# The order of two groups of projections at the start of a hybrid mixer: gates and attention values ahead of attention q and k

## The chip, the cores and the metric

The kernel runs on one core of one Trainium2 chip. The metric is device microseconds for one execution. Executions that are only timed give the median that is quoted; a profiled execution leaves a trace and has a time of its own, and the trace covers a span that is a little shorter than that time.

## The reference

The program computes a two-layer encoder trunk on 256 tokens of 1024 features in fp32. A layer is three residual steps, each followed by a LayerNorm: a SwiGLU feed-forward half-step, a mixer, and a second feed-forward half-step.

```python
for l in range(DEPTH):
    x = layer_norm(ALPHA * x + 0.5 * swiglu(x, ffn1_w_gu[l], ffn1_w_down[l]), ln1_g[l], ln1_b[l])
    h = x @ w_in[l]
    dq, dk, dv, mz, mxbc, mdt, gq, gk, gv, gz, gb, ga = jnp.split(h, IN_SPLITS, axis=-1)
    a_out = diff_attention_mixer(dq, dk, dv, cos, sin, da_lambda[l], da_subln_w[l], lambda_init(l))
    m_out = mamba2_mixer(mz, mxbc, mdt, ...)
    g_out = gated_deltanet_mixer(gq, gk, gv, gz, gb, ga, ...)
    mix = jnp.concatenate([a_out, m_out, g_out], -1) @ w_out[l]
    x = layer_norm(ALPHA * x + mix, ln2_g[l], ln2_b[l])
    x = layer_norm(ALPHA * x + 0.5 * swiglu(x, ffn2_w_gu[l], ffn2_w_down[l]), ln3_g[l], ln3_b[l])
```

The mixer has three head groups that read one projection `h`. Differential attention uses q and k (512 columns together) and values dv (256 columns): rotary embedding, two softmax maps per head, their difference times dv, and an RMS norm. The Mamba-2 group and the gated DeltaNet both use decays made from the gates (16 columns: `gb`, `ga`, `mdt`) through a sigmoid, a softplus and cumulative sums. The DeltaNet also needs normalised q and k, and inverts a triangular matrix for each chunk of 64 tokens.

## The kernel before, in words

The 256 tokens are two blocks of 128, b=0 and b=1. The program is six segments (feed-forward, mixer, feed-forward, twice). Each segment is a list of units, and a unit is one tile of weights: it is loaded by DMA from SP's queue into `raw` (5 buffers), split into a rounded high part `wh` on ACT (L265) and a remainder `wl` on DVE (L266) in 7 buffers each, and used on PE in three products, high x high, high x low and low x high. Token-stationary units do these at L357, L358 and L360 for one block at a time; units that serve both blocks at once do them at L342; the output and down projections at L253, L254 and L260.

The mixer's units come from the table `WIN`: each entry names a group of projections and its columns of `w_in`, and the list is worked in the order of the table. The groups `dqk` (512 wide: attention q and k) and `gd` (272 wide: dv and the gates, three DMAs to each part) have four parts each and are token-stationary; `qk0`, `qk1` (DeltaNet q and k), `m00` to `m11` (Mamba-2 x, B, C) and `v` (DeltaNet v) that follow serve both blocks at once; `mz`, `gz` and the output projection close the segment. Over the eight units of `dqk` and `gd`, `order()` lets block 0 run up to `LAG` = 5 units ahead of block 1, since block 1's input is ready later: the norm (L424 to L432) and the transposes `xps` (L275) that make `xT` for block 1 run while PE multiplies block 0.

When a group's last part is done, a generator is started (`spawn`) that issues the work on its result: `after_dqk` (L1018: rotary, transposes `dtps`, scores `scps`, exponentials `sm` at L1064, the sums of probabilities times dv in `dops`, norm into `do`), `after_gd` (L557: copies of dv and gates, then `decays`, L570, a chain of small DVE steps that ends in `a4` at L606, followed by the cumulative sums `csps` on PE and the decay matrices `dps` on PE, L647, with their exponentials `ex` on ACT, L652), and after `qk1` the DeltaNet's `delta`: SiLU of `qk` (L555), squares `sq`, sums `ssps`, `ss` (L693), r = ss^-0.5 on POOL (L695), factors `d` (L717, L718), products `laps` on PE and `LA` = laps x d x ex on DVE (L728). Generators are advanced between the units by their own estimates of time; a scheduler then fixes each engine's order at build time. Every engine works through its own list in that order: an instruction that waits holds all that stand behind it on its engine. The helpers record many operations from one line: L404 is every small matmul, L275 every transpose, L445 a power on POOL. PSUM has two pools of four buffers: `ps` for the units' sums, and `aux`, taken in turn, for all the mixers' small results, so that a new small result waits until the one four before it has been read.

## Time and profile before

| | |
|---|---|
| median of 3 timed executions | 1070.83 us (1070.76 to 1071.52) |
| the profiled execution: its time | 1073.73 us |
| its span in the trace | 1071.9 us, mean granted clock of TensorE 0.994 |
| PE busy | 1046.2 us (98%) |
| DVE busy | 754.8 us (70%) |
| ACT busy | 606.6 us (57%) |
| POOL busy | 30.6 us (3%) |

In the trace, busy time is that of instructions running; a bracket behind a row gives idle time before it and what ended this. Layer 1's mixer lies at about 187 to 357 us of the span, and layer 2's repeats it some 529 us later, wait for wait. In the page's 40 slices every slice but the first and the last has a busy PE share of 9 tenths or more.

### The profile page before, as it was taken

How to read it: one execution, taken by the hardware profiler on the slowest of the kernel's cores; microseconds unless marked ns; L12 is line 12 of the kernel's file. 1: busy time of each engine (PE TensorE's matmuls, PEld its weight loads, DVE VectorE, ACT ScalarE, POOL GpSimd, SP SyncE). 2: the span in 40 equal slices, each digit the busy share in tenths (PEclk: the TensorE clock that was granted, in tenths of full speed). 3: DMA queues.
4: the chain of work that ended last, by engine and by line, in shares of the span. 5: the costliest groups of instructions: out<-in, count | busy, mean ns of one | idle time of the engine just before them, and what ended most of it. 6: DMA issues, size and time to landing. Idle time of an engine off the chain costs nothing.

```text
span 1071.9 us, 17626 instructions
## 1 busy us (share of the span) xinstructions
PE 1046.2 (98%) x6358; PEld 894.5 (83%) x6358; DVE 754.8 (70%) x1554; ACT 606.6 (57%) x1301; POOL 30.6 (3%) x29
## 2 busy tenths in 40 slices
PE   8999999999999999999999999999999999999996
PEld 7888888788887788888878888887888878888885
DVE  6777754887877877774587776457977787777644
ACT  6687643487435566664456666435873445666530
POOL 0000000001001000000000000000010010000000
PEclk9999999999999999999999999999999999999999
DMA  9967664652334876666487665636522449666641
GB/s 294 292 180 203 196 193 143 178 158 64 113 100 138 236 207 188 195 193 189 133 247 202 182 192 183 193 108 188 163 73 80 148 134 263 184 190 187 197 134 40
DMA packets 221551, 184.42 MB, mean 172 GB/s; under 512 B 14608, under 2 KB 201368, under 8 KB 221464
## 3 DMA queue, kind: packets, MB, share of 16 engines
q1 hardware_dynamic: 221464, 183.30, 57.4%
q8 instruction: 50, 0.82, 0.3%
q14 instruction: 37, 0.30, 0.1%
HBM read 182.21 MB, written 1.05 MB: 171 GB/s over the span
## 4 chain that ended last, share of the span: by engine, by line
PE 84%; DVE 7%; ACT 4%; DMA 2%; issue 2%; POOL 1%; SPq 0%; DVEq 0%; POOLq 0%; ACTq 0%
PE ps L342 43%; PE po L253 7%; PE po L254 7%; PE po L260 7%; PE ps L360 4%; PE ps L357 4%; PE ps L358 4%; DVE wl L266 3%; DMA raw<-in_ffn_w_gu_dram 2%; PE ups L404 1%; PE gps L404 1%; ACT wh L265 1%; PE xps L275 1%; PE yps L404 1%; PE vnps L404 1%
## 5 line engine op out<-in xcount | busy, mean ns | idle before, releaser
L266 DVE TENSOR_TENSOR wl<-raw,wh 128x512 fp32r<-128x512 f32 (+1 forms) x672 | 437.6, 682 | 193.5 <-ACT wh L265 186.7
L265 ACT CAST wh<-raw 128x512 fp32r<-128x512 f32 (+1 forms) x672 | 386.2, 616 | 208.2 <-PE po L260 96.7
L342 PE MATMUL ps<-xT,wh 128*128 128x512 f32 (+1 forms) x1600 | 489.2, 365 | 0.0
L342 PE MATMUL ps<-xT,wl 128*128 128x256 f32 x1376 | 388.9, 283 | 0.0
L342 PEld LDWEIGHTS ps<-xT,wh 128*128 128x128 f32 x1600 | 287.7, 189 | 50.7 <-issue 0.7
L342 PEld LDWEIGHTS ps<-xT,wl 128*128 128x128 f32 x1376 | 261.5, 190 | 2.4 <-issue 2.0
L253 PE MATMUL po<-wh,hT 128*128 128x512 f32 x352 | 137.7, 391 | 0.0
L254 PE MATMUL po<-wl,hT 128*128 128x512 f32 x352 | 137.1, 389 | 0.0
L260 PE MATMUL po<-wh,hT 128*128 128x512 f32 x336 | 103.5, 389 | 0.0
L357 PE MATMUL ps<-wh,xT 128*128 128x512 f32 (+2 forms) x256 | 95.8, 379 | 1.1 <-ACT wh L265 1.0
L358 PE MATMUL ps<-wl,xT 128*128 128x512 f32 (+2 forms) x256 | 92.7, 369 | 0.5 <-DVE wl L266 0.5
L253 PEld LDWEIGHTS po<-wh,hT 128*128 128x128 f32 x352 | 66.1, 188 | 14.7 <-DVE hh L513 1.1
L254 PEld LDWEIGHTS po<-wl,hT 128*128 128x128 f32 x352 | 66.1, 188 | 13.4
L360 PE MATMUL ps<-wh,xT 128*128 128x512 f32 (+2 forms) x256 | 73.6, 371 | 1.1 <-DVE xT L266 1.1
L260 PEld LDWEIGHTS po<-wh,hT 128*128 128x128 f32 x336 | 63.1, 188 | 13.2
L265 ACT CAST hT<-hh 128x256 fp32r<-128x256 f32 x72 | 29.2, 406 | 70.3 <-DVE hh L515 70.3
L357 PEld LDWEIGHTS ps<-wh,xT 128*128 128x128 f32 x256 | 48.2, 188 | 10.8 <-ACT wh L265 1.9
L358 PEld LDWEIGHTS ps<-wl,xT 128*128 128x128 f32 x256 | 48.2, 188 | 8.2 <-DVE wl L266 1.2
L360 PEld LDWEIGHTS ps<-wh,xT 128*128 128x128 f32 x256 | 45.1, 188 | 9.6 <-DVE xT L266 2.0
L445 POOL TENSOR_TENSOR rsq<-rs,neghalf 128x1 f32<-128x1 f32 (+2 forms) x20 | 22.4, 1122 | 993.3 <-DVE rs L443 993.3
L514 ACT ACTIVATE ga<-ga 128x256 f32<-128x256 f32 x72 | 30.1, 418 | 35.9 <-DVE ga L511 35.9
L266 DVE TENSOR_TENSOR hT<-hh,hT 128x256 fp32r<-128x256 f32 x72 | 30.5, 424 | 26.0 <-ACT hT L265 26.0
(246 smaller groups left out, 918.1 us busy)
## 6 DMA issues: line engine op xcount, KB each, us to landing
raw<-in_ffn_w_gu_dram SPq DMA_DIRECT2D x350, 256.0 KB
raw<-in_ffn_w_down_dram SPq DMA_DIRECT2D x88, 512.0 KB
raw<-in_w_in_dram SPq DMA_DIRECT2D x40, 512.0 KB
raw<-in_w_out_dram SPq DMA_DIRECT2D x16, 512.0 KB
raw<-in_w_in_dram SPq DMA_DIRECT2D x24, 256.0 KB
g<-in_ln_g_dram SPq DMA_DIRECT2D x6, 512.0 KB
b<-in_ln_b_dram SPq DMA_DIRECT2D x6, 512.0 KB
x<-in_x_dram SPq DMA_DIRECT2D x4, 256.0 KB
```

Source lines behind the costliest of these rows:

```text
L253: mm(p, lhsT=xh, rhs=wh, start=start, stop=False)
L254: mm(p, lhsT=xh, rhs=wl, start=False, stop=False)
L260: mm(p, lhsT=xl, rhs=wh, start=False, stop=False)
L265: self.nc.scalar.copy(hi, src)
L266: self.nc.vector.tensor_tensor(lo, src, hi.bitcast(F32), op=ALU.subtract)
L342: self.nc.tensor.matmul(to, lhsT=a, rhs=r, start=first and n == 0, stop=end and n == len(mms) - 1, skip_group_check=True,)
L357: mm(ps, lhsT=x(kk)[:, 0], rhs=wh[:, s], start=u["part"] == 0 and kk == 0, stop=False)
L358: mm(ps, lhsT=x(kk)[:, 0], rhs=wl[:, s], start=False, stop=False)
L360: mm(ps, lhsT=x(kk)[:, 1], rhs=wh[:, s], start=False, stop=last and kk == ks - 1)
L404: self.nc.tensor.matmul(out, lhsT=lhsT, rhs=rhs, start=start, stop=stop)
L445: nc.gpsimd.tensor_tensor(r, t, self.neghalf[:, :n], op=ALU.pow)
L514: nc.scalar.activation(a, a, AF.Silu)
```

## The change

Two rows of the table `WIN` change places, in both layers.

```diff
 WIN = (
+    ("gd", ((512, 256), (3336, 8), (2304, 8)), None),
     ("dqk", ((0, 512),), None),
-    ("gd", ((512, 256), (3336, 8), (2304, 8)), None),
     ("qk0", ((2568, 128), (2312, 128)), (0, 128)),
     ("qk1", ((2696, 128), (2440, 128)), (0, 128)),
```

No instruction's arithmetic changes; where instructions stand does, at three places above all (all rows here are of layer 1).

**PE, the attention's scores of block 0.** Before, with `dqk` first, the score products (`scps`) stand between the units' wide products:

```order
L404 MATMUL scps_2240<-dkT_2215,dqT_2213 128x128
L357 MATMUL ps_2193<-wh_2038,xT_2136 128x512
L358 MATMUL ps_2193<-wl_2039,xT_2136 128x512
L357 MATMUL ps_2193<-wh_2038,xT_2136 128x512
L358 MATMUL ps_2193<-wl_2039,xT_2136 128x512
L360 MATMUL ps_2193<-wh_2038,xT_2136 128x512 x2
L404 MATMUL scps_2260<-dkT_2215,dqT_2213 128x128
L404 MATMUL scps_2261<-dkT_2215,dqT_2213 128x128
L404 MATMUL scps_2260<-dkT_2215,dqT_2213 128x128
L404 MATMUL scps_2261<-dkT_2215,dqT_2213 128x128
L360 MATMUL ps_2179<-wh_2122,xT_2136 128x272 x2
```

Now all token-stationary products are over when the first score product comes, and the cumulative sums (`csps`), both blocks' transposes and both blocks' scores stand close together, with a few products of `qk0` (L342) between:

```order
L404 MATMUL csps_2378<-a_990,cst 128x24 x2
L404 MATMUL csps_2378<-cst,a_990 128x128
L404 MATMUL scps_2390<-dkT_2361,dqT_2359 128x128
L404 MATMUL scps_2391<-dkT_2361,dqT_2359 128x128
L404 MATMUL scps_2390<-dkT_2361,dqT_2359 128x128
L404 MATMUL scps_2391<-dkT_2361,dqT_2359 128x128
L275 MATMUL dtps_2405<-cst,dqk_2338 128x128 x4
L404 MATMUL scps_2438<-dkT_2361,dqT_2359 128x128 x2
L342 MATMUL ps_2365<-xT_2098,wh_2254 128x256 x2
L342 MATMUL ps_2365<-xT_2098,wl_2255 128x256
L404 MATMUL scps_2439<-dkT_2361,dqT_2359 128x128 x2
L342 MATMUL ps_2365<-xT_2098,wh_2254 128x256 x2
```

The decay matrices (`dps`) of both blocks, which stood behind the scores, now stand partly among them and partly earlier among the products of `qk1` and `m00`.

**PE, the DeltaNet's norms and products.** Before, 3 and 13 products L342 and two pairs of decay matrices stand between the last sums `ssps` and the products `laps_2901`, which need a PSUM buffer that `LA` (L728) releases:

```order
L404 MATMUL ssps_2783<-cst,sq_2548 128x2 x6
L342 MATMUL ps_2957<-xT_2098,wh_2705 128x256
L342 MATMUL ps_2957<-xT_2098,wl_2706 128x256
L342 MATMUL ps_2957<-xT_2098,wh_2705 128x256
L647 MATMUL dps_2834<-ar_2781,css 128x512
L648 MATMUL dps_2834<-below,identr 128x512
L647 MATMUL dps_2853<-ar_2838,css 128x512
L648 MATMUL dps_2853<-below,identr 128x512
...
L342 MATMUL ps_2957<-xT_2098,wh_2705 128x256 x2
L404 MATMUL laps_2901<-qk_2547 128x256 x2
L404 MATMUL laps_2902<-qk_2547 128x256 x2
```

Now the decay matrices are done before, no product L342 stands between, and the transpose of the attention's result of block 1 (`mTps`) does:

```order
L404 MATMUL laps_2785<-qk_2531 128x256
L404 MATMUL ssps_2772<-cst,sq_2532 128x2 x6
L404 MATMUL laps_2785<-qk_2531 128x256
L404 MATMUL laps_2786<-qk_2531 128x256 x2
L275 MATMUL mTps_2807<-cst,do_2726 128x128 x2
L404 MATMUL laps_2901<-qk_2531 128x256 x2
L404 MATMUL laps_2902<-qk_2531 128x256 x2
L342 MATMUL ps_2844<-xT_2136,wh_2592 128x256
```

**DVE, the DeltaNet's factors.** Before, a remainder `wl` stands between the last factor (L718) and `LA`:

```order
L720 TENSOR_SCALAR rq_2879<-r_490_2794 128x8
L718 TENSOR_TENSOR d_2877<-d_2877,beta_2390 128x8
L266 TENSOR_TENSOR wl_2936<-raw_2622,wh_2935 128x512
L728 SCALAR_TENSOR_TENSOR LA_2884<-laps_2796,d_2877,ex_2601 128x256 x2
L728 SCALAR_TENSOR_TENSOR LA_2884<-laps_2797,d_2877,ex_2601 128x256 x2
```

Now the attention's result of block 0 (`mT`, L269), whose PSUM buffer `laps_2901` takes, stands there instead:

```order
L693 TENSOR_SCALAR ss_2781<-ssps_2772 128x16
L717 TENSOR_TENSOR d_2877<-r_490_2783 128x8
L719 TENSOR_TENSOR nk_2878<-r_490_2783,ss_2781 128x8
L720 TENSOR_SCALAR rq_2879<-r_490_2783 128x8
L718 TENSOR_TENSOR d_2877<-d_2877,beta_2252 128x8
L269 SCALAR_TENSOR_TENSOR mT_2766<-mTps_2767,nw,mT_2766 128x256
L728 SCALAR_TENSOR_TENSOR LA_2884<-laps_2785,d_2877,ex_2435 128x256 x2
L728 SCALAR_TENSOR_TENSOR LA_2884<-laps_2786,d_2877,ex_2435 128x256
```

Before, both blocks' `mT` of the attention (L269) stood ahead of L693. On ACT the number of table loads is the same, 20. Between the end of the projections of block 0's input and the start of `xps` for block 1, the split units are other ones: of ten remainders `wl` on DVE between block 0's and block 1's norms, four were 512 and six 272 wide; now six are 512 and four 272 wide.

## The prediction

> **What bounds the kernel now.** I read the page's first part, then the waits of PE, then each wait's place in PE's timeline, and last the chain and the clock at the longest.

> ```profile
> PE 1046.2 (98%) x6358; PEld 894.5 (83%) x6358; DVE 754.8 (70%) x1554; ACT 606.6 (57%) x1301; POOL 30.6 (3%) x29
> ```

> PE is idle for 1071.9 − 1046.2 = 25.7 us in all. The change adds and removes no product, so it can act only through PE's waits and its clock.

> ```profile
> PE laps L404 <- DVE LA L728: 4.3, 2, 2.1
> PE xps L275 <- DVE x L432: 2.9, 4, 0.8
> PE mTps L275 <- DVE go L829: 2.6, 2, 1.3
> PE mTps L275 <- ACT sm L1064: 2.5, 2, 1.2
> PE aps L275 <- DVE sm L1079: 0.4, 2, 0.2
> PE mTps L275 <- DVE do L1116: 0.2, 1, 0.2
> ```

> The columns are microseconds in all, times, and the longest. Five of these six lie wholly in the mixers, and of the `xps` waits two do, one in each layer. In layer 1 they stand at:

> ```profile
> 202.02 1.32 PE L275 MATMUL xps<-cst,x 128*128 128x128 f32 x8 [0.72 <-DVE x L432]
> ...
> 217.87 0.30 PE L275 MATMUL aps<-cst,sm 128*128 128x128 f32 x1 [0.22 <-DVE sm L1079]
> ...
> 228.86 0.44 PE L275 MATMUL mTps<-cst,do 128*128 128x128 f32 x2 [1.23 <-ACT sm L1064]
> ...
> 261.04 2.00 PE L404 MATMUL laps<-qk 64*128 64x256 f32 x8 [2.14 <-DVE LA L728]
> ...
> 334.47 0.63 PE L275 MATMUL mTps<-cst,go 128*128 128x128 f32 x4 [1.29 <-DVE go L829]
> ```

> So a mixer holds about 5.6 us of named waits, and each has its own cause. The dearest is `laps`; its chain, in order of time:

> ```profile
> 254.97 1.02 PE ssps L404 x9
> ...
> 256.01 0.19 DVE ss L693
> ...
> 256.27 2.91 POOL r L695
> ...
> 259.20 0.17 DVE d L717
> ...
> 259.60 0.60 DVE wl L266
> 260.20 0.80 DVE LA L728 x2
> ```

> POOL's power takes 2.91 us, and PE has products for only part of it. It costs more than its wait. Three windows show busy time of PE, PEld, DVE, ACT and POOL, then the granted clock:

> ```profile
> 258.80:261.00 2.20, 0.10 (x1) 0.00 (x0) 1.80 (x8) 2.20 (x6) 0.37 (x1) 1.00 0.00 0
> ...
> 261.20:264.60 3.40, 3.40 (x15) 2.61 (x16) 2.58 (x9) 1.38 (x3) 0.00 (x0) 0.50 0.00 0
> 264.60:266.00 1.40, 1.40 (x14) 1.40 (x13) 1.40 (x4) 1.14 (x2) 0.00 (x0) 1.00 0.00 0
> ```

> After the idle 2.2 us PE works at half clock for 3.4 us, which loses 3.4 × 0.5 = 1.7 us of work. The waits of 1.23 and 1.29 us leave the clock at 1.00. Somewhere between 1.3 and 2.1 us of idling, then, lies the point from which a wait costs 1.7 us more. [...]

> **The change part by part**, per layer; I take both layers as equal. Loads move too: gd's 12 small DMAs go ahead of dqk's four on SP's queue.

> ```profile
> 187.00:200.00 13.00, 12.82 (x64) 10.56 (x63) 12.96 (x28) 5.48 (x12) 0.92 (x1) 1.00 0.46 108
> ```

> Here the DMA share is 0.46 and no wait of PE names a weight's load; I count them at nothing. Were that cover gone, one tile late would show as a wait of PE for `wh`. The same row shows DVE busy for 12.96 of 13.00 us: this is the place where DVE, not PE, sets the time.

> (A) *The transposes of block 1.* They wait for DVE's norm, which stands behind remainders in DVE's list.

> ```profile
> 199.15 0.34 DVE wl L266
> ...
> 199.60 0.31 DVE wl L266
> ...
> 201.21 0.77 DVE x L432
> ```

> Ten remainders stand between the two norms; two of them change from 272 wide (0.34 us here) to 512 wide (0.60 us, the row at 259.60). That is 2 × (0.60 − 0.34) = +0.52. PE has the same products ahead of `xps` on both sides, 16 wide and 16 narrow, so the wait grows from 0.72 to 1.24 us: +0.52. The bound below is +0.2, if the earlier start of DVE on narrow ones wins some of it back.

> (B) *Waits that go.* `aps` (0.22) and the first `mTps` for `do` (1.23) came because the attention's chain ended while PE had nothing else in its list; now more products L342 stand ahead of them, as does the second `mTps` (0.22 in layer 1). 0.22 + 1.23 + 0.22 = −1.67. The nearest bounds are all of it, and −1.0, if a piece of the attention's chain is late anyway.

> (C) *Waits that come: the cluster of scores.*

> ```profile
> 212.37 1.28 ACT L1064 ACT_TABLE_LOAD   x1
> 213.66 0.37 ACT L1064 ACTIVATE sm<-scps,nmax 128x128 f32<-128x128 f32 x1
> ...
> 216.33 0.24 ACT L1064 ACTIVATION_READ_ACCUMULATOR sm<-scps,nmax 128x1 f32 x1
> ...
> 220.40 0.38 ACT L1039 ACTIVATE dqT<-dtps 128x256 f32<-128x256 f32 x1
> 220.68 0.37 ACT L1043 COPY dkT<-dtps 128x256 f32<-128x256 f32 x1
> ...
> 229.30 2.75 PE ps L342 x23
> ```

> Block 0's eight exponentials take ACT from 213.66 to 216.57, 2.9 us, and the two copies behind `dtps` 0.65 us. Before, wide unit products covered them. Now PE's scores of block 1 wait for aux buffers that these exponentials read. Between the first `scps` and block 1's third pair stand 13 products L342, at 2.75/23 = 0.12 us each: 1.6 us. If PE's own small work covered nothing, the rest would be 2.9 + 0.65 − 1.6 = 2.0 us; `csps`, which stands behind a chain of some fifteen small DVE steps, could add 0.4: upper bound 2.4. Lower bound 0: the small products themselves cover all. Pair by pair (two exponentials 0.72 us, against one score pair and three to six L342 products) I find only 0.1 us or so at each of three or four places, and 0.5 at `csps`: I take +0.85, nearer to the lower end since PE's small work does run while ACT does.

> (D) *`laps`.* The chain from `ssps` is the same, but what covers it is not. Before, 16 products L342 and two pairs of `dps` stood behind `ssps`; now only a pass of `laps` and one `mTps` do.

> ```profile
> L269 DVE SCALAR_TENSOR_TENSOR mT<-mTps,nw,mT 128x256 fp32r<-128x256 f32 x12 | 5.8, 481 | 0.4 <-ACT mT L268 0.3
> ```

> `laps` of block 1 now waits for the buffer that L269 reads, and L269 stands in DVE's list behind L718, so behind POOL. From the end of `ssps` (255.99): 0.28 to POOL's start, 2.91, 0.42 to the end of the small factors (259.60, where the remainder stood), 0.48 for L269 = 4.09 us. PE meanwhile has three products of `laps`, which at half clock took 2.00 for four pairs and so take 0.25 each at full, and two transposes, some 0.3: about 1.05. The wait is 3.04 instead of 2.14: +0.9. The upper bound is +1.3 (the transposes run under the products and PE's work is 0.65); the lower +0.5, if the rest of `ssps` comes apart and 0.4 of it lies behind POOL's start. The half clock behind it stays, since both waits are above 2.1 us: no change.

> (E) *ACT ahead of it.* Before `sq` is whole, ACT now loads tables four times in a row.

> ```profile
> L555 ACT ACT_TABLE_LOAD x6 | 7.7, 1283 | 0.1
> ...
> L652 ACT ACTIVATE ex<-dps 128x512 f32<-128x512 f32 x12 | 6.8, 610 | 0.0
> L652 ACT ACT_TABLE_LOAD x4 | 5.1, 1283 | 0.1
> ...
> L677 ACT ACTIVATE sq<-qk 128x512 f32<-128x512 f32 x2 | 1.2, 619 | 0.0
> ```

> Four loads at 1.28 are 5.1; two `qk`, two `sq`, four `ex` and one `dsq` at about 0.48 net are 4.3; together 9.4 us. PE meanwhile has 73 products L342, 8.7 us, and small ones for 1.8: 10.5. So it is covered, by 1.1 us: 0. [...] The row at 212.37 has its first exponential 0.01 us after the load's end; it shows the load and no drain behind it.

> (F) *The end of the mixer.* The inversion starts when 17 more products are done, 17 × 0.12 = 2.0 us later, and the products of `m` that it had beside it are done earlier, so the last `mTps` (1.29) has one product of the output projection less ahead of it.

> ```profile
> 335.17 0.39 PE L253 MATMUL po<-wh,mT 128*128 128x512 f32 x1
> 335.40 0.39 PE L254 MATMUL po<-wl,mT 128*128 128x512 f32 x1
> ```

> Starts lie 0.23 apart: +0.23. Bounds −1.29 (a chain that ends early enough) and +0.5.

> Sum: 0.52 − 1.67 + 0.85 + 0.9 + 0 + 0.23 = +0.83 per layer, +1.7 for two. The profiled execution took 1073.73 us with a span of 1071.9; it would take 1075.4. The median, 1070.83, is 2.9 below that execution, so I add the difference to it: 1072.5 us. What this measurement can tell from no change is about 0.2%, 2.1 us: below 1068.7 counts as faster, above 1073.0 as slower.

> **The rivals.**

> *The softmax holds PE (slower).* PE's list is kept in order, so each late exponential holds all of `qk0`'s products behind it. If (C) is at its upper bound, a layer has +0.83 + 1.55 = 2.4, two 4.8: 1075.6 us. For it: the wait of 1.69 us of ACT for `nmax` in the same region, where ACT and DVE hand each pair on:

> ```profile
> 227.78 0.47 ACT L1064 ACTIVATE sm<-scps,nmax 128x256 f32<-128x256 f32 x1 [1.69 <-DVE nmax L1061]
> ```

> Against it: the table load ahead of the exponentials goes, as the decays load it. It decides from where two exponentials and their maxima take longer than what PE has between two pairs.

> *The same, with the clock (slower).* If those waits run together to over 2.1 us, another 1.7 per layer is lost: 4.8 + 3.4 = +8.2, 1079.0 us. Against it: small products stand between the waits, and 1.23 us of pure idling left the clock at 1.00. [...]

> *`laps` is freed (faster).* If `ssps` ends early against PE's list, because ACT's chain of (E) is shorter than I make it and the scheduler's order holds PE elsewhere, the wait falls under 1.3 us and the clock stays full: −0.9 from 2.14 and −1.7 of clock instead of +0.9, so 0.83 − 0.9 − 0.9 − 1.7 = −2.7 per layer, 1065.5 us. For it: all decay matrices are made before. Against it: POOL's 2.91 us stands between two steps that PE's list now puts next to each other, so nothing can cover it.

> *The waits only change places.* (C) at 0 and (D) at +0.5 give −0.4 per layer: 1070.0 us. It is within the forecast's own range.

> **How the numbers follow.** The forecast with its own range, 1069.7 to 1074.0, has 0.52; softmax holds PE 0.24; with the clock 0.11; `laps` freed 0.13. Within 0.2% fall 0.43 of the forecast's 0.52 and 0.02 of the second: 0.45. Slower: 0.07 of the forecast, 0.22 and 0.11: 0.40. Faster: 0.13 and 0.02 of the forecast: 0.15. The range goes from 1068.5 to 1077.0, which leaves out nearly all of the freed `laps` and most of the case with the clock, and holds the upper bound of (C) with some of (D)'s.

> **What would show it.** (A) is right if the `xps` wait in a mixer is 1.1 to 1.4 us; (B) if the waits for L1064 and L1079 by `mTps` and `aps` are gone; (C) by new waits of PE at `csps`, `scps` and `dps` of together under 1.2 us a layer; (D) if the wait at `laps` is 2.8 to 3.4 us, named after L269 or its neighbour, with the clock at 0.50 behind it; (E) if `ssps` has no wait; (F) by 1.3 to 1.8 us before the last `mTps`. The prediction falls if `laps` waits under 1.3 us, if `ssps` waits for `sq` on ACT, or if a window around the scores has a clock under 1.00.

## The result and the profile after

The changed kernel takes 1078.39 us (median of 3 executions, 1077.68 to 1079.73), against 1070.83 before: 1.0064 times as long, with a 95% interval of 1.0048 to 1.0081. It is slower by 7.6 us, and lies above the predicted range, which ended at 1077.0. The profiled execution took 1079.73 us with a span of 1078.0 us and a mean granted clock of 0.990; before it was 0.994.

The page's first part, after the change:

```profile
PE 1053.7 (98%) x6358; PEld 899.8 (83%) x6358; DVE 753.5 (70%) x1554; ACT 605.9 (56%) x1301; POOL 31.3 (3%) x29
```

PE idles for 1078.0 − 1053.7 = 24.3 us, which is 1.4 less than before. Its busy time is up by 7.5 us, although it works on the same 6358 products. The waits fell, as a sum, and the products took longer. That is the main reading of this case: the loss doesn't stand in the list of waits.

PE's waits in the changed kernel (microseconds in all, times, the longest):

```profile
PE laps L404 <- DVE mT L269: 4.6, 2, 2.3
PE xps L275 <- DVE x L432: 3.8, 4, 1.2
PE mTps L275 <- DVE go L829: 2.3, 2, 1.2
PE csps L404 <- DVE a L606: 0.4, 2, 0.2
```

The waits for `sm` and `do` are gone, a small one at `csps` has come, and `laps` waits hardly longer than before.

Where the time lies by stage: the first transposes of a segment mark its start. A mixer is the stretch from its own first `xps` to that of the feed-forward behind it. For that stretch of layer 1, the view by windows gives length, then busy time of PE, PEld, DVE, ACT and POOL, then the granted clock. Before:

```profile
192.76:347.44 154.68, 148.54 (x1250) 129.48 (x1249) 122.32 (x295) 92.03 (x211) 11.34 (x8) 0.99 0.43 129
721.56:876.16 154.60, 148.51 (x1249) 129.50 (x1248) 122.31 (x295) 92.02 (x211) 11.33 (x8) 0.99 0.43 129
```

After:

```profile
195.38:352.80 157.42, 152.48 (x1250) 131.78 (x1248) 122.96 (x294) 93.51 (x211) 11.65 (x8) 0.98 0.42 125
725.12:882.23 157.11, 152.15 (x1249) 131.49 (x1248) 122.95 (x294) 93.54 (x211) 11.71 (x8) 0.98 0.42 126
```

Layer 1's mixer is 2.74 us longer, layer 2's 2.51. In layer 1 PE's idle time fell from 6.14 to 4.94 us (−1.20), and its busy time rose by 3.94. The other 0.8 of the spans' difference of 6.1 us lies outside the mixers: the start of the program took 2.6 us more in this one execution (195.38 against 192.76; a later execution of the same kernel has 192.74), and the two feed-forwards between the mixers took 374.12 us before (721.56 − 347.44) and 372.32 after (725.12 − 352.80). The 372.4 of a later profile of the changed kernel and the 374.2 of one with a filler show that this stretch goes up and down between executions, so it is not counted to the change.

Which products took longer: PE's groups by shape over the whole program, with busy time in all and the mean duration of one in ns. Before:

```profile
L404 PE MATMUL scps<-dkT,dqT 32*128 32x256 f32 x32 | 4.4, 406 | 0.0
L404 PE MATMUL scps<-dkT,dqT 32*128 32x128 f32 x32 | 2.9, 296 | 0.0
L404 PE MATMUL laps<-qk 64*128 64x256 f32 x32 | 6.5, 514 | 4.3 <-DVE LA L728 4.3
```

After:

```profile
L404 PE MATMUL scps<-dkT,dqT 32*128 32x256 f32 x32 | 6.8, 400 | 0.0
L404 PE MATMUL scps<-dkT,dqT 32*128 32x128 f32 x32 | 4.2, 295 | 0.0
L404 PE MATMUL laps<-qk 64*128 64x256 f32 x32 | 10.2, 541 | 4.6 <-DVE mT L269 4.6
```

Read the mean beside the sum. One wide score product lasts the same 0.40 us in both kernels. Before, 32 of them are 32 × 0.406 = 13.0 us of product within 4.4 us of busy time: three are under way at a time. After, 32 × 0.400 = 12.8 us lie in 6.8 us: fewer than two. The score products cost 2.4 + 1.3 = 3.7 us more over two layers, and `laps` another 3.7. With 1.2 us less idling per layer, that is 3.7 − 1.2 = 2.5 of the 2.6 us per layer; what is left is small and of both signs.

PE's timeline in layer 1's mixer, after the change (start, length, and in brackets the idle time before it):

```profile
205.01 1.32 PE L275 MATMUL xps<-cst,x 128*128 128x128 f32 x8 [1.17 <-DVE x L432]
...
226.01 1.15 PE L404 MATMUL scps<-dkT,dqT 32*128 32x256 f32 x8
...
228.33 1.12 PE L404 MATMUL scps<-dkT,dqT 32*128 32x256 f32 x4
...
231.49 1.13 PE L404 MATMUL scps<-dkT,dqT 32*128 32x256 f32 x4
...
256.12 1.50 PE L404 MATMUL ssps<-cst,sq 128*128 128x2 f32 x12
...
258.94 0.44 PE L275 MATMUL mTps<-cst,do 128*128 128x128 f32 x2
261.69 2.92 PE L404 MATMUL laps<-qk 64*128 64x256 f32 x8 [2.31 <-DVE mT L269]
```

Here the loss in the scores can be seen directly. A group of eight records that stand together takes 1.15 us. The other group is torn in two, with products L342 between, and each half of four takes 1.12 or 1.13 us: half the work for the same time. Before, all sixteen stood together:

```profile
221.66 2.19 PE L404 MATMUL scps<-dkT,dqT 32*128 32x256 f32 x16
```

Each half writes one of two PSUM buffers. The score products of one buffer read one strip of 32 partitions of their operands, those of the other buffer another strip; the rows above give these products as 32*128; the trace has those of L342 as 128*128.

And the clock behind `laps`, in four windows of the changed kernel:

```profile
256.70:260.10 3.40, 2.68 (x17) 1.99 (x16) 0.17 (x1) 1.44 (x4) 2.19 (x1) 1.00 0.00 0
260.10:263.50 3.40, 1.81 (x6) 1.59 (x7) 2.66 (x10) 2.73 (x6) 0.71 (x1) 0.51 0.00 0
263.50:267.00 3.50, 3.50 (x15) 2.80 (x13) 3.50 (x9) 0.00 (x0) 0.00 (x0) 0.50 0.17 25
267.00:270.40 3.40, 3.40 (x31) 3.40 (x30) 2.90 (x7) 3.16 (x6) 0.00 (x0) 1.00 0.36 129
```

The half clock holds for two stretches of 3.4 us, 6.8 in all, where it held for one before. It also begins sooner: PE goes idle at 259.38, when `mTps` ends, and the clock falls at about 260.1, some 0.8 us later. Before, that took 2.3 us (from 258.9 to 261.2). Layer 2 has two stretches as well, 0.50 from 789.22 to 796.03; there PE goes idle at 789.13 and the clock falls at 789.21, so hardly any idling stands ahead of the fall.

### The profile page after: what moved, and what is told of

It reads as the page before. It is cut to its first block, busy times and chain, and to the rows that moved or that the text cites. A ratio compares the mean times of both kernels' runs of the same rounds, so it can differ in the third digit from the quotient of the medians.

```text
span 1078.0 us, 17661 instructions
## 1 busy us (share of the span) xinstructions
PE 1053.7 (98%) x6358; PEld 899.8 (83%) x6358; DVE 753.5 (70%) x1554; ACT 605.9 (56%) x1301; POOL 31.3 (3%) x29
## 3 DMA queue, kind: packets, MB, share of 16 engines
HBM read 182.21 MB, written 1.05 MB: 170 GB/s over the span
## 4 chain that ended last, share of the span: by engine, by line
PE 89%; DVE 6%; issue 1%; DMA 1%; POOL 1%; ACT 0%; SPq 0%; DVEq 0%
PE ps L342 45%; PE po L253 7%; PE po L254 7%; PE po L260 7%; PE ps L360 4%; PE ps L357 4%; PE ps L358 4%; DVE wl L266 2%; DMA raw<-in_ffn_w_gu_dram 1%; PE gps L404 1%; PE ups L404 1%; PE scps L404 1%; DVE x L424 1%; PE xps L275 1%; DVE x L432 1%
## 5 line engine op out<-in xcount | busy, mean ns | idle before, releaser
L266 DVE TENSOR_TENSOR wl<-raw,wh 128x512 fp32r<-128x512 f32 (+1 forms) x672 | 436.8, 680 | 192.2 <-ACT wh L265 179.0
L342 PE MATMUL ps<-xT,wh 128*128 128x512 f32 (+1 forms) x1600 | 489.8, 365 | 0.0
L342 PE MATMUL ps<-xT,wl 128*128 128x256 f32 x1376 | 387.8, 282 | 0.0
L342 PEld LDWEIGHTS ps<-xT,wh 128*128 128x128 f32 x1600 | 287.5, 189 | 53.0 <-issue 3.3
L342 PEld LDWEIGHTS ps<-xT,wl 128*128 128x128 f32 x1376 | 261.5, 190 | 0.4
L253 PE MATMUL po<-wh,hT 128*128 128x512 f32 x352 | 137.7, 391 | 0.0
L254 PE MATMUL po<-wl,hT 128*128 128x512 f32 x352 | 137.0, 389 | 0.0
L253 PEld LDWEIGHTS po<-wh,hT 128*128 128x128 f32 x352 | 66.1, 188 | 14.6 <-DVE hh L513 1.1
L254 PEld LDWEIGHTS po<-wl,hT 128*128 128x128 f32 x352 | 66.1, 188 | 13.4
L266 DVE TENSOR_TENSOR hT<-hh,hT 128x256 fp32r<-128x256 f32 x72 | 30.5, 424 | 26.0 <-ACT hT L265 26.0
```

The lines of the kernel that those rows point to most:

```text
L253: mm(p, lhsT=xh, rhs=wh, start=start, stop=False)
L254: mm(p, lhsT=xh, rhs=wl, start=False, stop=False)
L266: self.nc.vector.tensor_tensor(lo, src, hi.bitcast(F32), op=ALU.subtract)
L342: self.nc.tensor.matmul(to, lhsT=a, rhs=r, start=first and n == 0, stop=end and n == len(mms) - 1, skip_group_check=True,)
```

## The experiments

The expectations number the runs e1 to e12, in the order in which they stand here. They name theories by letters. P says that the neighbourhood of PE's small products is the cost: score products, and `laps`, of different strips run beside each other only where they stand together. N is what was left of P after e1: they do so as long as no product that uses more rows stands between them. C says that the clock is the cost: the gap at `laps` now costs two stretches of half clock, and the rest is small. W says that PE waits for the exponentials on ACT. In each batch the kernel before ran on the same chip. The ratios are those on record, each with its 95% interval; they are not the ratio of the two medians. None of the twelve runs leaves work out; products that are added write zeros or values that are overwritten.

### Scores and `laps` of the kernel before, tile after tile

```diff
+            with self.tc.manual_schedule(engines={PE}):
-            for j in range(2):
                 for i in range(2):
+                    for j in range(2):
                         o = slice(32 * (i0 + i), 32 * (i0 + i) + 32)
                         self.mm(pis[i][:, j * nk : (j + 1) * nk], ...)
```

(and the same for `laps`)

> The kernel before, with one thing changed: the score products and the products of laps are issued one PSUM tile after the other (both products into the first tile, then both into the second) instead of alternating between the two tiles, whose operands lie in different row strips. Nothing is left out. Theory P (pairs: two products in different row strips of PE run side by side when they are neighbours in its list, and the changed kernel tore such neighbours apart): in the trace of after, four score products torn apart take 1.05 us (256 wide) or 0.62 us (128 wide), where neighbours take about half; with all 16 + 16 apart, scores cost 2.1 + 1.2 = 3.3 us more and laps 1.0 to 1.5 more per layer: +4.3 to +4.8 per layer, about 1080 us. Theory C (only the longer stretch of half clock behind laps costs) and theory W (waits for the exponentials on ACT, as the second rival of the prediction had it): no wait and no idle stretch changes here, 1070.5 to 1072.

Measured: a median of 1071.86 us against 1072.44 before, ratio 1.0002 (0.9993 to 1.0012). The group in the profile:

```profile
L404 PE MATMUL scps<-dkT,dqT 32*128 32x256 f32 x32 | 4.6, 400 | 0.1
```

It stays at 4.6 us. So the two tiles need not alternate product by product; that form of the theory falls. It says nothing yet of products that are pulled apart by others.

### The changed kernel, both buffers claimed ahead of each group

```diff
+            with self.tc.manual_schedule(engines={PE}):
+                self.nc.tensor.matmul(pis[0][:, 0:2], lhsT=self.zero, rhs=self.zero[:, 0:2], start=True, stop=True)
+                self.nc.tensor.matmul(pis[1][:, 0:2], lhsT=self.zero, rhs=self.zero[:, 0:2], start=True, stop=True)
                 for j in range(2):
                     for i in range(2):
```

(and the same ahead of `laps`). A product of two columns takes the wait for each PSUM buffer on itself; the four real products behind it then stand together. The order of the table `WIN` stays changed.

> The changed kernel; ahead of each group of four score products and of four laps products two tiny products (2 columns of zeros) touch both PSUM tiles first, so that both buffers are waited for there and the four products stand together and alternate again. Nothing is left out, 12 tiny products a layer are added (about 0.1 us each with the switch, +1.2 a layer at most). Theory P: -1.7 for the scores and -0.5 to -1.5 for laps, +0.5 to +1.2 for the tiny products: -1 to -2.5 per layer, 1073.5 to 1076.5 us. Theory C: the idle stretch stays, so 1078.4 and up to +2. Theory W: the waits come earlier (for the later of both buffers) and stay: 1078.4 or more.

Measured: 1070.16 us (1069.04 to 1074.51), 0.9988 (0.9976 to 1.0001). The whole loss is gone, which is more than any of the theories gave (the best was 1073.5), and no execution but one lost noticeable clock: nine have 0.997 to 0.999. Groups in the profile:

```profile
L404 PE MATMUL laps<-qk 64*128 64x256 f32 x32 | 4.5, 402 | 0.0
L404 PE MATMUL scps<-dkT,dqT 32*128 32x256 f32 x32 | 4.5, 400 | 0.0
L404 PE MATMUL scps<-dkT,dqT 32*128 32x128 f32 x32 | 2.9, 296 | 0.0
L701 PE MATMUL laps<-zero 128*128 128x2 f32 x8 | 1.3, 235 | 2.9 <-DVE mT L269 2.9
```

The scores are back at 4.5 and 2.9 us and `laps` is at 4.5. The wait fell from 2.31 to some 1.45 us: in the order that the scheduler made of this, 22 products L342 (some 2.6 us) stand between `ssps` and block 1's `laps`, where the changed kernel has none. So three things changed together: scores, `laps`, and the gap. The next runs part them.

### Filling the gap with zero products, in both kernels

```diff
+            if b == 1:
+                with self.tc.manual_schedule(engines={PE}):
+                    for _ in range(9):
+                        nc.tensor.matmul(pss[:, 128:256], lhsT=self.zero, rhs=self.zero, start=True, stop=True)
             for j in range(2):
```

> The changed kernel with nine products of zeros (128 x 128) in PE's list ahead of block 1's laps, where PE sat idle for 2.31 us; they write a corner of PSUM that nobody reads. Theory C: half clock lasted 6.83 us in each layer, 1.5 of it idle, so 2.6 us of work were lost; with the gap filled the clock stays at 1.00: -2.6 per layer, about 1073 us. Theory P: the torn scores stay; only block 1's laps stand together again: -0.3 per layer, 1077.5 to 1078.4.

> The kernel before with the same nine products of zeros ahead of block 1's laps, where PE sat idle for 2.14 us. If idling is what halves the clock there (3.41 us at half, 1.7 us of work lost per layer): -1.7 per layer, about 1067.5 us, and clock 1.00 around laps in the trace. If products of zeros don't count as work for the clock, or the clock follows something else: 1070.5 to 1071.5.

Measured: on the change 1082.01 us (1.0104, 1.0089 to 1.0119), on the kernel before 1075.72 (1.0042, 1.0027 to 1.0056). Both miss. PE's waits in the first of them:

```profile
PE mTps L275 <- DVE mT L269: 6.2, 2, 3.1
```

and its timeline in layer 1, around the zero products (L702):

```profile
258.81 0.66 PE L275 MATMUL mTps<-cst,do 128*128 128x128 f32 x2 [3.09 <-DVE mT L269]
259.26 4.05 PE L702 MATMUL ssps<-zero 128*128 128x128 f32 x18
263.24 1.17 PE L404 MATMUL laps<-qk 64*128 64x256 f32 x8
```

In the second, the wait for `LA`, 2.2 us in each layer, now stands at `dps`. The zero products wrote into the tile of `ssps` and so held its PSUM buffer; the wait moved ahead of them, and they ran behind the gap, not in it. So these two are no test of what a filled gap does to the clock. They do show what a PSUM buffer held for longer costs here, and the last row of the timeline that eight records of `laps`, nearly all at full clock, take 1.17 us.

### The changed kernel once more, and with a filler that holds no buffer

The first is the changed kernel as it is. The second adds eight products of zeros into a sum of the units that is open anyway (the tile of zeros `nil` and the name `open` for that sum are set up elsewhere in the edit):

```diff
+                    for _ in range(8):
+                        nc.tensor.matmul(self.open[:, 0:P], lhsT=self.nil, rhs=self.nil, start=False, stop=False, ...)
```

> The changed kernel itself, unaltered, so that what follows is compared on one chip: 1077.5 to 1081 us, with half clock for two windows of 3.41 us behind laps in each layer. If the long stretch at half clock was an accident of that one profiled execution, its trace shows one window here and the time comes nearer to 1075.

> The changed kernel with eight products of zeros that add nothing to the sum that PE has open (its own tile of zeros, no PSUM buffer held longer): seven stand in PE's list between the transposes and block 1's laps, where PE sat idle for 2.31 us, and fill about 1.7 us of it; block 1's four laps products stand as neighbours. Theory C (clock): 6.83 us at half clock, 1.56 of them idle, lost 2.6 us a layer; with the clock at 1.00 that is -5.2 in all, about 1073 us; if only one of the two windows goes, 1075 to 1076.6. If zeros don't keep the clock up, or if the clock isn't what costs: 1077.5 to 1081, as e5.

Measured: 1078.23 us (1.0062, 1.0045 to 1.0080), with a clock of 0.990 or 0.991 in each of four executions; so the loss is no accident of one execution. With the filler 1079.19 (1076.84 to 1083.25; 1.0077, 1.0046 to 1.0107). In its profile layer 1's mixer has no half clock at all and still takes 156.9 us, only 0.7 less than the change alone. PE's waits:

```profile
PE laps L408 <- DVE mT L272: 2.0, 2, 1.0
...
PE laps L408 <- DVE LA L739: 0.9, 2, 0.4
PE gps L408 <- DVE T L890: 0.8, 1, 0.8
```

The gap has been filled by work that nobody needs, `laps` still waits 1.0 us behind the filler, and new waits come for `LA` (0.4 us in each layer) and `T` (0.8 us in layer 1). Layer 2 does have one stretch at half clock and takes 157.7. Keeping the clock up is thus worth little as long as the chain through POOL still stands in PE's way; and layer 1, at full clock, is still 2.2 us longer than before (156.9 against 154.7). The new waits are 1.3 of this, so the clock is not the whole cause, but this run doesn't price the rest.

### `laps` alone claimed, in both kernels

The edit of the second experiment, ahead of `laps` only, with the table of constants as operand.

> The changed kernel with the tiny products (2 columns) ahead of the laps products alone; the scores stay torn apart. The order lets some eleven products L342 slip in between: three ahead of ssps, four behind it, four between the tiny products of block 1, so that the idle stretch shrinks from 2.31 to about 1.5 us. Theory C: clock 1.00 around laps, -2.6 a layer, the wait -0.8 and +0.6 for the tiny products: -2.8 a layer, about 1073 us. If instead e2 was fast because of the scores (theory N: score products are cheap only as neighbours), this one stays at 1076 to 1079 with the scores at 3.2 and 1.9 us a layer in the trace as in after. Both together: 1073 here against 1070 in e2 less the price of its tiny score products.

> The kernel before with the same tiny products ahead of laps: some eight products L342 slip in between block 1's, so that its idle stretch shrinks from 2.14 to about 1.2 us. Theory C: the clock stays at 1.00, -1.7 a layer, wait -0.9, +0.5 for the tiny products: -2.1 a layer, about 4 us under the kernel before. If the clock doesn't follow the idle stretch: within 1 us of before.

Measured: on the change 1076.44 us (1073.12 to 1085.37; 1.0050, 1.0024 to 1.0076); on the kernel before 1073.79 (1.0018, 1.0006 to 1.0029). Groups and waits, first of the changed kernel:

```profile
L404 PE MATMUL laps<-qk 64*128 64x256 f32 x32 | 4.9, 426 | 0.0
L700 PE MATMUL laps<-cst 128*128 128x2 f32 x8 | 1.3, 235 | 4.1 <-DVE mT L269 4.1
```

then of the kernel before:

```profile
L404 PE MATMUL laps<-qk 64*128 64x256 f32 x32 | 5.1, 415 | 0.0
L700 PE MATMUL laps<-cst 128*128 128x2 f32 x8 | 1.5, 256 | 4.3 <-DVE LA L731 4.3
```

On the change the median is 1.8 us lower, less than a third of the loss, and the two intervals overlap (1.0045 to 1.0080 without the claim). `laps` fell from 10.2 to 4.9 us, the scores' line reads 6.8 and 400 as in the changed kernel, and the wait at `laps` is still 2.1 us where 1.5 was expected. On the kernel before it was expected to gain and lost: `laps` takes 1.4 us less over two layers, the tiny products take 2.8 (1.5 in the line shown and 1.3 in that of the other buffer), and the wait of 2.1 us stayed. A claim pays only where it mends something.

The second profile shows something else. PE idles for 2.14 us ahead of `laps` in both layers, exactly as in the kernel before, and the clock never falls:

```profile
257.50:264.30 6.80, 4.66 (x37) 4.07 (x36) 4.67 (x16) 6.37 (x12) 1.95 (x1) 1.00 0.00 0
```

So the same idle time goes with a stretch of half clock in one profile and with none in another. In the kernel before with zero products it differs within one execution: 2.21 us of idling are followed by a stretch in layer 2 and by none in layer 1. The length of the gap alone does not decide it.

### Scores of the kernel before torn on purpose, and a control

One tiny product is put between the two tiles' score products; the control has the same tiny product ahead of them. In both, the products are issued tile after tile, which cost nothing in the first experiment.

```diff
+            with self.tc.manual_schedule(engines={PE}):
                 for i in range(2):
+                    if i == 1:      # the control: i == 0
+                        self.nc.tensor.matmul(pis[1][:, 0:2], lhsT=self.cst[:, 0:P], rhs=self.cst[:, 0:2], ...)
+                    for j in range(2):
```

> The kernel before; each group of four score products is issued tile after tile, with one tiny product over all 128 rows (2 columns, overwritten behind it) between the two tiles' products. To be compared with e10, which has the same tiny product ahead of the group. Theory N (score products of two tiles run side by side only while nothing with more rows stands between them): the 256 wide groups take 2.1 instead of 1.07 us, the 128 wide 1.25 instead of 0.64: +3.3 us a layer in the trace over e10, 6 us in the time if nothing else is late there. If the torn scores of after were slow for another reason (waits for the exponentials that the records count as busy), the groups take 1.1 and 0.7 us as in e10 and the times agree within 1 us.

> The control of e9: the kernel before, tile after tile, with the tiny product ahead of each group of four score products. Neighbours stay neighbours: groups at 1.07 and 0.64 us as in before and e1, four tiny products at about 0.1 to 0.2 us a layer: +0.4 to +0.8 a layer, 1072 to 1074 us where the kernel before has 1071.5 to 1072.5.

Measured: torn 1080.95 us (1077.45 to 1081.51; 1.0077, 1.0053 to 1.0101), control 1072.27 (1.0004, 0.9994 to 1.0014). The place of a product of two columns makes 8.7 us, where 6 were expected. Groups of the torn kernel:

```profile
L404 PE MATMUL scps<-dkT,dqT 32*128 32x256 f32 x32 | 8.0, 444 | 0.0
L404 PE MATMUL scps<-dkT,dqT 32*128 32x128 f32 x32 | 5.7, 296 | 0.0
```

and of the control:

```profile
L404 PE MATMUL scps<-dkT,dqT 32*128 32x256 f32 x32 | 4.6, 400 | 0.0
L404 PE MATMUL scps<-dkT,dqT 32*128 32x128 f32 x32 | 2.9, 296 | 0.0
```

The narrow products, whose own duration is the same 296 ns in both, take 5.7 instead of 2.9 us: 32 × 0.296 = 9.5 us of product, 3.3 under way at a time in the control and 1.7 in the torn kernel. PE waits for nothing in either (the last column is 0.0). This is the cost that the changed kernel has at its torn groups, shown with only the place of the tiny product changed. The groups' own busy time is 6.2 us more over two layers, part of it at half clock (the wide products' mean rose from 400 to 444 ns); the rest of the 8.7 us stands beside a clock that is lost, as shown below, and is not split further. That the tiny product writes the second tile, and not that it stands between, could be a rival; the changed kernel rules it out, since there products L342 that write other buffers stand between, and each half takes the same 1.12 or 1.13 us. In this kernel, then, the products of two strips run beside each other where they stand together, and one product over all 128 rows between them is enough to end it.

The torn kernel's timeline shows how it comes about:

```profile
223.63 1.13 PE L404 MATMUL scps<-dkT,dqT 32*128 32x256 f32 x4
...
225.00 1.14 PE L404 MATMUL scps<-dkT,dqT 32*128 32x256 f32 x8
```

Four records of one strip alone take 1.13 us. The eight behind the first tiny product are four of one strip and four of another, and take 1.14: the second four cost nothing while the first run.

The clock in the same place, windows of the torn kernel:

```profile
223.00:226.40 3.40, 3.40 (x23) 2.48 (x22) 2.60 (x12) 3.40 (x11) 0.00 (x0) 1.00 0.99 319
226.40:229.80 3.40, 3.40 (x12) 2.56 (x12) 2.21 (x11) 0.88 (x2) 1.02 (x1) 0.51 0.63 220
229.80:233.20 3.40, 3.40 (x17) 3.40 (x17) 3.40 (x11) 2.52 (x9) 0.00 (x0) 0.50 0.01 2
```

and the second of them in the control:

```profile
226.40:229.80 3.40, 2.89 (x25) 2.69 (x24) 2.54 (x8) 2.88 (x9) 0.83 (x1) 1.00 0.44 150
```

The torn kernel loses the clock for 6.8 us here (for 3.4 us at the same place of layer 2) though PE is recorded as busy for the whole of the 3.4 us ahead of it; the control idles for 0.5 us in this window and keeps it.

### The changed kernel with both claims on other operands, and with the claim of the scores alone

The second experiment's edit with the constants as operand; then its part at the scores alone.

> e2 again, with the constants' tile in place of the tile of zeros as the tiny products' operands, so that it differs from e7 in the scores alone. If e2's gain was the order it gave (neighbours, and products L342 beside POOL's power): 1070 to 1071 us and no half clock, as e2. If it came from holding the tile of zeros: 1074 to 1077, as e7.

> The changed kernel with the tiny products ahead of the scores alone. The scores are neighbours again (-1.7 a layer) and pay for it with the tiny products (+1.7). Its order also moves some products L342 between ssps and laps. Theory C (the stretch at laps, with its wait and its two windows at half clock, is most of the loss): faster than e5 only by what becomes of that stretch: 1072 to 1075 if the idle stretch falls under 1.5 us and no more than one window a layer is at half clock, 1077.5 to 1079 if the stretch stays. Theory N (the torn scores are most of it): it can't gain more than the tiny products cost, 1077 to 1079 whatever laps does.

Measured: both claims 1072.17 us (1070.53 to 1073.51; 1.0004, 0.9994 to 1.0015); scores alone 1080.57 (1071.27 to 1083.97; 1.0069, 1.0040 to 1.0097).

The first lies 2 us above the second experiment and below the 1074 to 1077 expected if the tile of zeros had made the gain. It doesn't keep the clock everywhere, as it was expected to, and so gives a price of the clock. Its layer 1 has one stretch at half clock and takes 154.83 us from first transpose to first transpose, its layer 2 has none and takes 153.42; the second experiment, with none in either, took 153.34 and 153.31. One stretch of 3.4 us costs 154.83 − 153.4 = about 1.4 us here. Other profiles with a stretch in one layer alone give 1.5 (`laps` claimed in the changed kernel, 156.06 against 154.55), 1.3 (zero products in the kernel before, 156.59 against 155.27) and 0.1 (the first experiment, 153.89 against 153.82): there the stretch lies ahead of the wait for POOL, which shrank from 1.9 to 0.3 us and took it in. The gap ahead of `laps` is the same in both layers of the run with both claims, 1.47 and 1.45 us; one is followed by a stretch and the other isn't.

The second fits neither theory by its median. It has scores together and `laps` torn, and its ten executions spread over 12.7 us in step with the granted clock: 1071.27 and 1071.95 us at 0.998, 1074.30 at 0.993, and 1080.27 to 1083.97 at 0.984 to 0.987. It is one kernel with one order of instructions. In the profiled one (clock 0.993) layer 1's mixer keeps the clock and takes 154.00 us; layer 2's loses it for three stretches, 10.2 us, and takes 157.79. Two windows of its profile, at the same place of either layer:

```profile
250.00:260.00 10.00, 9.32 (x55) 7.14 (x54) 5.26 (x21) 6.69 (x15) 4.02 (x2) 1.00 0.01 5
780.00:790.00 10.00, 10.00 (x36) 7.35 (x35) 7.21 (x22) 3.58 (x7) 3.01 (x1) 0.60 0.14 37
```

PE is recorded busy for 10.00 of 10 us and runs at 0.60 of its clock. In the two executions at 0.998 the loss is gone (1071.3 and 1072.0 us). Only the profiled execution has a trace, so where the seven at 0.984 to 0.987 lose the clock is not shown. The scores are not all that this run mends: in its order products L342 stand between `ssps` and `laps`, and the wait at `laps` fell to 0.7 us in layer 1 and to none in layer 2.

No kernel tried here is clearly better than the kernel before: the best, with both claims, is 0.9988 in one batch and 1.0004 in the other.

## Why the prediction was wrong

The forecast was +0.83 us per layer; the profile shows +2.6. The direction in which it leaned was right, the size was not, and the two pieces that were missed have different causes. The step that failed stands at the head of the working: that the change “can act only through PE's waits and its clock”, since it adds and removes no product. There is a third way, how many products are under way at a time, and it had no term in the sum. The runs put it at 1.85 us a layer for the scores, under (C), and about 0.8 for block 0's `laps`, under (D). Beside it failed the sentence that the half clock stays as it was.

**(A) was right.** The `xps` wait of the mixer is 1.17 us, against the predicted 1.24.

**(B) was right.** The waits for L1064, L1079 and the second `mTps` are gone, all 1.67 us.

**(C) failed, in its cause and in its size.** It looked for waits of PE for ACT's exponentials, took 0.85 us, and named 2.4 as the upper bound. Such waits are not in the trace: only `csps` waits, for 0.2 us. What took their place is the torn score products: (6.8 + 4.2 − 4.4 − 2.9) / 2 = 1.85 us a layer, recorded as busy time. The order of instructions quoted ahead of the prediction already shows it: `scps_2438` and `scps_2439` with products L342 between, where the kernel before has all four neighbouring. The experiment with the torn scores and its control show that this alone costs time. That the scheduler tears them because one of two PSUM buffers comes free before the other is argued from the order; that claiming both buffers ahead puts them together again and takes their busy time back to 4.5 and 2.9 us is shown.

**(D) failed in its cover and at its last sentence.** The wait was taken as 3.04 us and is 2.31. The chain:

```profile
257.65 0.19 DVE ss L693
...
257.91 2.91 POOL r L695
...
261.17 0.07 DVE d L718
261.23 0.41 DVE mT L269
```

From `ssps`' end at about 257.63 to the end of L269 at 261.64 are 4.01 us, as predicted (4.09); what was mis-sized is the cover. It was put at 1.05 us and is 259.38 − 257.63 = 1.75, since `laps` of block 0 is torn by `ssps` and runs slowly: 6 records take 1.47 us where 8 together took 1.17. So part of the lateness that was to be a wait became busy time. Another part is a wait that the list can't show: block 1's `laps` write two buffers, the first freed by L269 at 261.64, the second, by its turn in `aux`, by the second of the three `LA` behind L269, which ends at 262.42. The records of the second tile start at 262.56, 0.88 us after those of the first (261.69), and PE counts as busy with the first meanwhile. Before, both tiles started together, at 261.04 and 261.05. That makes the 2.92 us of this group against 2.00, both at half clock; it is read from the order and the times, and no run was made for it alone.

“The half clock behind it stays” failed too: it holds for two stretches in place of one. By work, an estimate, (6.8 − 1.55 of idling) × 0.5 = 2.6 us are lost where it was 1.7: some 0.9 more. The reasoning was that a wait above 2.1 us sets the clock back once. The clock fell 0.8 us after the idling began in layer 1 and 0.1 us after in layer 2, and ahead of the gap stand `laps`, with 64 of 128 rows, and `ssps`, with two columns each. That this work counts too is read from the traces; no run was made for it alone. Nor is there a point “between 1.3 and 2.1 us of idling” from which a wait costs a stretch: 2.14 us cost none in the kernel before with `laps` claimed, and 1.47 us were followed by one in layer 1 of the run with both claims.

**(E) was right.** `ssps` has no wait. The four table loads cost nothing here.

**(F) had the wrong sign, and is small:** 1.17 us before the last `mTps` instead of 1.29, where 1.52 was expected.

**The sum, by measured terms,** per layer from the two windows of layer 1: −1.20 of idle time (+0.45 `xps`, +0.17 `laps`, +0.22 `csps`, −0.12 `mTps` for `go`, −1.67 and smaller ones), +1.9 for the scores, +1.7 for `laps` (0.8 in block 0, 0.9 in block 1), +0.3 for the rest of PE's work: +2.7. At most some 0.9 of the last two are the extra stretch at half clock. Two layers make 5.2 us in the profiles. The medians differ by 7.6, and the clock would account for this too: later executions of the kernel before have a mean clock of 0.993 to 0.999, most above that of its profile (0.994), those of the change 0.990 or 0.991 throughout. One stretch fewer than in the profile of before (1.4 us) and a feed-forward without the 1.8 us more that this profile has would account for the gap between it (1073.73) and the median (1070.83); so the mixers' 5.2 and that one stretch are 6.6 us, where the later batch measured 6.7 (1078.23 against 1071.54). Adding a difference of profiles to a median whose executions have other clocks was the last weak step.

**The rivals.** “The same, with the clock” gave 1079.0 us and is nearest to the result. Its mechanism was half right: another 1.7 us a layer was to be lost to the clock, but among the scores, by waits that run together. The clock was lost at `laps`, and the scores lost time of another kind. It had a chance of 0.11; the argument against it, that 1.23 us of pure idling left the clock at 1.00, took idle time for the only thing that counts. “The softmax holds PE” has the right place and nearly the right size (1075.6), and the wrong cause.

## What to carry to other kernels

The products on 32 rows were cheap only in company here (32 records in 2.9 us together, in 5.7 torn): when an order is changed, look whether groups on different row strips still stand together, and what their PSUM buffers wait for. The profile of the change has its loss in busy time (7.5 us more, with 1.4 us less of idling), so compare each group's busy time with count times mean duration, and the start-to-start length of a stage, before reading waits. The gap of 2.31 us behind products of 64 rows and of two columns came with 6.8 us at half clock, so compare executions at the same granted clock, and never add a difference of two profiles to a median without it.
